# The first gate of a fused transformer kernel: its 16 modulation steps on ScalarE and GpSimd instead of TensorE

## The chip, the cores and the metric

The kernel runs on one core of a Trainium2 chip. The metric is device time in microseconds (us) for one execution of the whole program. The kernel before takes 2242.73 us (median of three runs, 2242.59 to 2245.43).

A core has five engines, each with an instruction queue that is worked off strictly in order: TensorE (PE, matrix products; PEld is its weight load), VectorE (DVE), ScalarE (ACT), GpSimd (POOL) and SyncE (SP, which here only issues DMA transfers). An instruction whose input is not ready holds up everything behind it in its queue.

## The reference, cut to what matters

The program is three transformer layers on 256 tokens of width 2048. Only the first is touched here, and in it only the first gate, `gt1`:

```python
ada = silu(c) @ w_ada + b_ada                 # c: (1, 2048), w_ada: (2048, 6*2048)
sh1, sc1, gt1, sh2, sc2, gt2 = split(ada, 6)
h   = rmsnorm(x, norm1_g) * (1 + sc1) + sh1
proj = h @ w_in                               # 2048 x 3664: q, k, v, index heads, pool
...attention and pooling...
x   = x + gt1 * (mix @ w_out)
h2  = rmsnorm(x, norm2_g) * (1 + sc2) + sh2
x   = x + gt2 * mixture_of_experts(h2)
```

So `gt1` is a row of 2048 numbers: a vector of 2048 times a 2048 x 2048 matrix (16 MB of float32), plus a bias. It is needed on all 128 partitions, since it multiplies the rows of the tokens.

## The kernel before, in words

**Steps.** The first layer is a list of steps (`Dense` objects) that `run_steps` (line 81) goes through. A step has a `first` part (issue the DMA of its weights, and for a projection cast them to a rounded half on ACT), an `end` part (the remainder on DVE) and a `step` part (the products on PE). `first` and `end` are done two steps ahead of `step`. After each step `bg.tick()` emits one piece of each kind of background work: the indexer, the choice of the 64 best keys (`choose`), normed and rotated q and k (`qk_ready`), pooling, attention, and at the end whatever was handed to `bg.later`, one piece of it at every tick.

**Projections.** A projection step (`dense_tok`, lines 489 on; its products are recorded on line 578, its cast on 526, its remainder on 167 like every `tensor_tensor`) takes two blocks of 128 input rows by 512 columns. Each operand is split in a rounded half `h` and a remainder `l`, and three products are made for each of two token halves, 12 in all. Two steps share one load of 1 MB. There are three buffers for the halves (`hp`, line 289), so a cast waits until PE is done with the step three back.

**Modulation steps.** An `ada_step(q, k)` loads one slab, 128 partitions by 2048 columns (1 MB, line 314), and adds `silu(c)` times the slab to a PSUM bank with four matmuls (line 321), side by side on four column groups of 32. A group is 16 steps; `q` is 2 for `gt1`, 3 and 4 for the second shift and scale, 5 for `gt2`. After the sixteenth step of `gt1`, `row` adds the bias and `spread` (line 398) puts the row on all partitions with four matmuls, when the attention phase starts.

**Order.** `merge` lays the modulation steps between projection steps: first `rows[3]` and `rows[4]` (the last two input blocks of the first five column chunks), then `wide` (24 steps for columns 1024 to 1535 and 2640 to 3663), then the 32 steps of `out_steps`, which multiply with `w_out` and need `gt1`.

**Buffers.** All these loads, projection or modulation, take their place from one ring, `raw()` (lines 262 on). In the middle of this phase it has six places of 1 MB: three buffers `w`, the two halves of the tile `X`, and `wx`. From the first step of the last eight of `wide` on it has four, `w, w, w, wx` (line 968), because `X` is about to be loaded again with the tokens; when `attention()` is called, at the end of `wide`, it gets six again with the halves of `big`. SP issues the loads in order: a load waits until its place is free, and all loads behind it wait too.

## Time and profile before

| | |
|---|---|
| median of three runs | 2242.73 us |
| profiled execution: its own time | 2241.87 us |
| its span (first to last instruction) | 2240.1 us |
| PE busy over the span | 1902.8 us (85%) |
| DVE, ACT, POOL busy | 989.3, 629.7, 73.4 us |
| moved by DMA | 694.94 MB |

The page of the profile cuts the span in 40 slices of 56 us. The steps of `gt1` lie in slices 3 to 5 (155 to 232 us) in the kernel before. Slices 11 to 24 are the experts of the first layer, and there the DMA runs at a constant 421 GB/s; from slice 25 on the second and third layers run, which the change doesn't touch. A row of a timeline gives start, duration, engine, source line, operation, the tile written and the tiles read, shape and count, and in brackets how long the engine had sat idle before and what it waited for.

### The profile page before, as it was taken

To read this page: it belongs to the slowest core of one execution; us is meant where nothing else is said; L and a number is where in the kernel's file an instruction comes from. 1 tells how busy PE (TensorE), PEld (TensorE's weight loads), DVE (VectorE), ACT (ScalarE), POOL (GpSimd) and SP (SyncE) were. 2 spreads that over 40 slices of the span, in tenths; PEclk is the share of its full clock that TensorE was granted. 3 is DMA by queue.
4 is the path that set the end of the run, shared out by engine and by line. 5 is a ranking of instruction groups with operands and counts; after the bars stand their busy time and mean duration, and the time that the engine had idled before them with its cause. 6 is when DMAs were issued, how large, how long until landed. Compare 5 with 4: busy or idle time off the path is not lost.

```text
span 2240.1 us, 35046 instructions
## 1 busy us (share of the span) xinstructions
PE 1902.8 (85%) x14718; PEld 1371.0 (61%) x14718; DVE 989.3 (44%) x1866; ACT 629.7 (28%) x1072; POOL 73.4 (3%) x90
## 2 busy tenths in 40 slices
PE   5999999986678676766767685999999999999998
PEld 3666656752234142423233242799989999989986
DVE  2456736531112121121212121667886657556864
ACT  2333324320000000000000010365574444435543
POOL 2000100000000000000000000000000011200000
PEclk9999999998799788898878788999999999999999
DMA  9999898899899999999999999855535556444554
GB/s 334 382 361 339 314 393 295 331 378 416 351 421 421 420 421 421 421 421 421 420 421 418 421 415 421 309 170 175 184 128 177 181 168 182 148 151 151 170 189 149
DMA packets 198065, 694.94 MB, mean 310 GB/s; under 512 B 20454, under 2 KB 44552, under 8 KB 140432
## 3 DMA queue, kind: packets, MB, share of 16 engines
q1 hardware_dynamic: 194608, 682.03, 80.0%
q0 software_dynamic: 2000, 6.89, 1.0%
q10 hardware_dynamic: 1296, 3.74, 0.5%
q8 instruction: 117, 1.92, 0.3%
q14 instruction: 44, 0.36, 0.0%
HBM read 690.49 MB, written 2.11 MB: 309 GB/s over the span
## 4 chain that ended last, share of the span: by engine, by line
PE 41%; DMA 28%; DVE 2%; ACT 1%; issue 1%; SPq 0%; ACTq 0%; POOLq 0%; POOL 0%; DVEq 0%
PE acc L578 29%; DMA w<-in_w_dram 12%; DMA a<-in_w_dram 9%; PE acc L1151 4%; PE acc L1186 3%; DMA wx<-in_w_dram 3%; DMA h<-in_w_dram 2%; PE acc L1216 1%; DVE Og L167 1%; DMA w<-in_l_w_uq_dram 1%; PE acc L1378 1%; PE tps L818 1%; PE tps L781 1%; DMA w<-in_l_w_in_dram 0%; PE tps L1712 0%
## 5 line engine op out<-in xcount | busy, mean ns | idle before, releaser
L578 PE MATMUL acc<-h,h 128*128 128x512 f32 (+1 forms) x1152 | 274.7, 388 | 11.5 <-ACT h L526 4.2
L1186 PE MATMUL acc<-w,Xg 128*32 128x256 f32 x2048 | 213.2, 462 | 66.3 <-DMA w<-in_w_dram 64.7
L578 PEld LDWEIGHTS acc<-h,h 128*128 128x128 f32 x1152 | 203.1, 190 | 87.5 <-issue 21.5
L167 DVE TENSOR_TENSOR s<-s,acc 64x256 f32<-64x256 f32 (+1 forms) x34 | 14.9, 439 | 414.1 <-ACT s L1193 409.7
L1186 PEld LDWEIGHTS acc<-w,Xg 128*32 128x32 f32 x2048 | 91.1, 128 | 163.9 <-DMA w<-in_w_dram 93.2
L167 DVE TENSOR_TENSOR Og<-acc,gt 32x512 f32<-32x512 f32 x124 | 85.2, 687 | 219.9 <-PE acc L1216 218.3
L1193 ACT ACTIVATE s<-acc 64x256 f32<-64x256 f32 x32 | 12.1, 377 | 599.5 <-PE acc L1186 599.5
L1186 PE MATMUL acc<-a,Xg 128*32 128x256 f32 x1408 | 136.1, 452 | 46.2 <-DMA a<-in_w_dram 44.0
L167 DVE TENSOR_TENSOR h<-w,h 128x1024 fp32r<-128x1024 f32 (+2 forms) x104 | 121.6, 1173 | 64.1 <-ACT h L526 63.9
L526 ACT CAST h<-w 128x1024 fp32r<-128x1024 f32 (+2 forms) x104 | 103.6, 1002 | 110.9 <-PE acc L578 51.2
L1186 PEld LDWEIGHTS acc<-a,Xg 128*32 128x32 f32 x1408 | 59.0, 126 | 108.9 <-DMA a<-in_w_dram 60.4
L578 PE MATMUL acc<-a,w 128*128 128x256 f32 x948 | 122.1, 285 | 0.1
L578 PE MATMUL acc<-a,wx 128*128 128x256 f32 x948 | 121.8, 284 | 0.2 <-DVE wx L167 0.2
L1151 PE MATMUL acc<-Ps,x 128*128 128x128 f32 x448 | 100.3, 396 | 25.0 <-DVE Ps L1139 21.8
L578 PE MATMUL acc<-a,h 128*128 128x256 f32 (+1 forms) x924 | 118.8, 284 | 0.4 <-DVE h L167 0.4
L1216 PE MATMUL acc<-w,aT 128*32 128x512 f32 x600 | 83.0, 650 | 42.1 <-DMA w<-in_w_dram 26.0
L1151 PEld LDWEIGHTS acc<-Ps,x 128*128 128x128 f32 x448 | 98.5, 310 | 33.1 <-issue 33.1
L578 PEld LDWEIGHTS acc<-a,wx 128*128 128x128 f32 x948 | 116.4, 191 | 2.5 <-issue 2.0
L578 PEld LDWEIGHTS acc<-a,w 128*128 128x128 f32 x948 | 116.6, 191 | 1.8 <-issue 0.7
L578 PEld LDWEIGHTS acc<-a,h 128*128 128x128 f32 (+1 forms) x924 | 113.5, 191 | 2.1 <-issue 1.3
L578 PE MATMUL acc<-a,gt 128*128 128x256 f32 (+1 forms) x876 | 112.3, 284 | 0.0
L578 PEld LDWEIGHTS acc<-a,gt 128*128 128x128 f32 (+1 forms) x876 | 107.6, 191 | 1.8 <-issue 1.7
(496 smaller groups left out, 2819.6 us busy)
## 6 DMA issues: line engine op xcount, KB each, us to landing
w<-in_w_dram SPq DMA_DIRECT2D x206, 1024.0 KB, 19.8
a<-in_w_dram SPq DMA_DIRECT2D x116, 1024.0 KB, 19.8
w<-in_l_w_in_dram SPq DMA_DIRECT2D x160, 512.0 KB, 4.6
w<-in_w_ada_dram SPq DMA_DIRECT2D x44, 1024.0 KB, 7.6
w<-in_l_w_out_dram SPq DMA_DIRECT2D x64, 512.0 KB, 4.7
h<-in_w_dram SPq DMA_DIRECT2D x29, 1024.0 KB, 19.8
wx<-in_w_dram SPq DMA_DIRECT2D x29, 1024.0 KB, 19.8
w<-in_w_ada_dram SPq DMA_DIRECT2D x30, 512.0 KB, 9.8
```

The lines of the kernel that those rows point to most:

```text
L167: (e or DVE).tensor_tensor(out=o, in0=x, in1=y, op=op)
L526: ACT.copy(h, t)
L578: PE.matmul(out_of(r), lt, rt, start=first and i == 0 and o == 0, stop=last and i == 2, skip_group_check=True)
L781: PE.transpose(p[:, b * 128:(b + 1) * 128], P[h][:, b * 128:(b + 1) * 128], ident)
L818: PE.matmul(p[:, r], q[:, t * 128:(t + 1) * 128], k[:, 0:128 * (t + 1)], start=True, stop=True)
L1151: PE.matmul(b[:, (k - k0) * 128:(k - k0 + 1) * 128], x1[:, t, k:D:16], flat(Ps)[:, t], start=t == 0, stop=t == 1)
L1186: PE.matmul(p1[32 * j:32 * j + 32, 0:256], Xg[:, k, 32 * el:32 * el + 32], w[:, k % 4, (j % 2) * 256:(j % 2) * 256 + 256], start=k == 0, s ...
L1193: ACT.activation(s[0:64], p1[0:64, 0:256], AF.Silu)
L1216: PE.matmul(p2[32 * j:32 * j + 32, :], aT[:, kk % 2, (kk // 2) * 32:(kk // 2) * 32 + 32], down[kk][:, j * 512:(j + 1) * 512], start=kk == ...
L1378: PE.matmul(p, PWT[:, t * 128:(t + 1) * 128], Og[:, n:n + 512], start=True, stop=True)
```

## The change

The 16 steps of `gt1` no longer use PE. Such a step, `gate_step(k)`, loads the same slab of 1 MB through the same ring. Then ACT makes copies of it in eight pieces of 256 columns, each scaled by `silu(c)` of its partition, into two small buffers that are used in turn (`some`; it goes by the name `sel`), and POOL adds each piece to a tile `gt1` of 128 x 2048. The first two pieces come with the step, two more with every tick: so four in the step's own turn, two in the next, two in the one after. At the end the 128 partitions of `gt1` are summed, and the sum put on all of them, by one product with ones (`spread_sum`, four matmuls as before).

The order changes with it: the steps of the other groups (`ada`) are laid at half the rate, and the 16 new steps, `g1`, between: 2 with `rows[3]`, 3 with `rows[4]`, 11 in `wide`. Before the end of `wide` there were 32 modulation steps on PE and are now 17; in the first half of `out_steps` 18 and now 16, in the second 3 and now 4. The selector `sel` is made where `gt2` is spread, not at the start. All loads are still made, each once.

```diff
-        sel = pp.tile([128, 4, 128], F32, name="sel")
         DVE.memset(kc["ones"], 1.0)
-        DVE.memset(sel, 0.0)
-        for j in range(4):
-            DVE.memset(sel[32 * j:32 * j + 1, j], 1.0)
...
+        some = pp.tile([128, 2, 256], F32, name="sel")
+
+        def gate_step(k):
+
+
+            cell = {}
+
+            def prep():
+                cell["w"] = w = raw().rearrange("p k n -> p (k n)")
+                SP.dma_start(w, wada[:, k, 2 * D:3 * D])
+
+            def pieces_of(g, w):
+                for i in range(8):
+                    x, n = some[:, i % 2], slice(256 * i, 256 * i + 256)
+                    ACT.activation(x, w[:, n], AF.Copy, scale=cs[:, k:k + 1])
+                    tt(g[:, n], g[:, n], x, OP.add, POOL)
+                    if i % 2:
+                        yield
+
+            def step():
+                if k == 0:
+                    gate["gt1"] = g = pe.tile([128, D], F32, name="gt1")
+                    POOL.memset(g, 0.0)
+                    POOL.dma_start(g[0:1, :], a["b_ada"][0:1, 2 * D:3 * D])
+                bg.later(pieces_of(gate["gt1"], cell["w"]))
+            return Dense(prep, step)
+
+        def spread_sum(name):
+
+            g = gate[name]
+            for j in range(4):
+                t = tps()
+                PE.matmul(t, kc["ones"], g[:, j * 512:(j + 1) * 512], start=True, stop=True)
+                evac(g[:, j * 512:(j + 1) * 512], t)
+                yield
+
...
-        ada = [ada_step(2, k, row("gt1", lambda: pe.tile([128, 512], F32, name="grow"))) for k in range(16)]
-        ada += [ada_step(3, k, columns(2, lambda: ())) for k in range(16)]
+        g1 = [gate_step(k) for k in range(16)]
+        ada = [ada_step(3, k, columns(2, lambda: ())) for k in range(16)]
...
-        bias_row(2, pe.tile([128, 512], F32, name="brow"))
...
-        order += merge(rows[2], lead[3][3:] + lead[4][:3]) + merge(rows[3], lead[4][3:]) + ada[:2]
+        order += merge(rows[2], lead[3][3:] + lead[4][:3]) + merge(rows[3], lead[4][3:] + g1[:2]) + ada[:2]
         del ada[:2]
-        order += merge(rows[4], ada, 6)
+        order += merge(merge(rows[4], ada, 3), g1[2:5])
...
-        order += merge(wide, ada, 24)
+        order += merge(merge(wide, ada, 12), g1[5:])
...
-            for g in (pool_means(4), pool_mix(), spread("gt1", lambda: gt1_at().rearrange("p t c -> p (t c)")),
+            for g in (pool_means(4), pool_mix(), spread_sum("gt1"),
...
-        order += merge(out_steps[:16], ada, 18) + merge(out_steps[16:], ada, len(ada) - TAIL)
+        order += merge(out_steps[:16], ada, 16) + merge(out_steps[16:], ada, len(ada) - TAIL)
...
+                        next(turn_gate)
                         weights()
```

Three places show how the queues change. Each row is a source line, an operation with the tile written and the tiles read, and the queues that it waits for; a number behind a tile tells one use of a buffer from the next, `in_w_ada_dram` is a modulation load, `in_w_in_dram` a load of `wide`, and `in_w_out_dram` the first load of `out_steps`.

SP, before, from the second-last load of `wide` to the first load of `out_steps`:

```order
L517 DMA w_2226<-in_w_in_dram 128x4x512 [waits DMAHW3_49,PE_49]
L314 DMA w_2243<-in_w_ada_dram 128x2048 [waits DMAHW4_49,DVE_49]
L314 DMA w_2264<-in_w_ada_dram 128x2048 [waits DMAHW5_49,DMAHW1_49,PE_49]
L517 DMA wx<-in_w_in_dram 128x4x512 [waits DMAHW6_49,PE_49]
L314 DMA w_2287<-in_w_ada_dram 128x2048 [waits DMAHW7_49,DVE_49]
L314 DMA w_2308<-in_w_ada_dram 128x2048 [waits DMAHW0_49,PE_49]
L314 DMA w_2314<-in_w_ada_dram 128x2048 [waits DMAHW1_49,PE_49]
L314 DMA wx<-in_w_ada_dram 128x2048 [waits DMAHW2_49,DVE_49]
L989 DMA X<-in_x_dram 128x2x2048
L314 DMA w_2347<-in_w_ada_dram 128x2048 [waits DMAHW3_49,PE_49]
L517 DMA big<-in_w_out_dram 128x4x512
```

SP, after, the same stretch (line 392 is a load of the new `gate_step`, line 310 of another modulation step, 554 a projection):

```order
L554 DMA w_2388<-in_w_in_dram 128x4x512 [waits DMAHW4_49,Activation_49]
L310 DMA w_2408<-in_w_ada_dram 128x2048 [waits DMAHW5_49,DMAHW1_49,DVE_49]
L392 DMA w_2426<-in_w_ada_dram 128x2048 [waits DMAHW6_49,PE_49]
L554 DMA wx<-in_w_in_dram 128x4x512 [waits DMAHW7_49,Activation_49]
L310 DMA w_2472<-in_w_ada_dram 128x2048 [waits DMAHW0_49,DVE_49]
L392 DMA w_2497<-in_w_ada_dram 128x2048 [waits DMAHW1_49,PE_49]
L310 DMA w_2517<-in_w_ada_dram 128x2048 [waits DMAHW2_49,Activation_49]
L310 DMA wx<-in_w_ada_dram 128x2048 [waits DMAHW3_49,DVE_49]
L1025 DMA X<-in_x_dram 128x2x2048
L310 DMA w_2543<-in_w_ada_dram 128x2048 [waits DMAHW4_49,PE_49]
L554 DMA big<-in_w_out_dram 128x4x512
```

The last two loads of `wide`, and the load `w_2517` that stands ahead of the tokens and of `w_out`, waited for PE and now wait for ACT (Activation): their places were those of new steps.

ACT, before, the casts of the last three loads of `wide` (two casts each) and of the first of `out_steps`:

```order
L526 CAST h<-w_2176 128x1024 [waits DVE_49]
L526 CAST h<-w_2226 128x1024 [waits DMAHW7_49,DVE_49]
L526 CAST h<-w_2226 128x1024 [waits DVE_49,PE_49]
L526 CAST h<-wx 128x1024 [waits DMAHW2_49,DVE_49,PE_49]
L526 CAST h<-wx 128x1024 [waits DVE_49,PE_49]
L153 COPY PP<-acc 128x512 [waits PE_49]
L153 COPY qiT<-tps 128x512 [waits PE_49]
L526 CAST h<-big 128x1024 [waits DMAHW1_49,DVE_49]
```

ACT, after, the same stretch (line 397 is a scaled piece):

```order
L563 CAST h<-w_2326 128x1024 [waits DVE_49]
L397 ACTIVATE sel<-w_2306,cs 128x256 [waits DMAHW4_49,Pool_49]
L397 ACTIVATE sel<-w_2306,cs 128x256 [waits Pool_49] x7
L563 CAST h<-w_2388 128x1024 [waits DMAHW0_49,DVE_49]
L563 CAST h<-w_2388 128x1024 [waits DVE_49,PE_49]
L397 ACTIVATE sel<-wx,cs 128x256 [waits DMAHW7_49,Pool_49]
L397 ACTIVATE sel<-wx,cs 128x256 [waits Pool_49] x7
L563 CAST h<-wx 128x1024 [waits DMAHW3_49,DVE_49,PE_49]
L563 CAST h<-wx 128x1024 [waits DVE_49,PE_49]
L397 ACTIVATE sel<-w_2426,cs 128x256 [waits DMAHW2_49,Pool_49]
L397 ACTIVATE sel<-w_2426,cs 128x256 [waits Pool_49] x5
L153 COPY PP<-acc 128x512 [waits PE_49]
```

Between the casts of two loads stand eight pieces, and each of these waits for POOL.

ACT, before, where `rows[4]` begins: the last modulated block of tokens (`h_6` and `h_7`) and the casts of the first two steps of `rows[4]` (`w_1269`):

```order
L153 COPY arow<-ada 128x256
L526 CAST h<-w_1269 128x1024
L157 ACTIVATE rl<-h_6_244,shsck,gsc 128x256
L424 CAST h_6_1288<-rl 128x512
L526 CAST h<-w_1269 128x1024
L157 ACTIVATE rl<-h_7_251,shsck,gsc 128x256
L424 CAST h_7_1302<-rl 128x512
```

ACT, after, the same place; the first cast of `rows[4]` is the last row, and the slabs of the first two new steps are `w_1217` and `X`:

```order
L153 COPY arow<-ada 128x256
L563 CAST h<-wx 128x1024
L157 ACTIVATE rl<-h_6_236,shsck,gsc 128x256
L461 CAST h_6_1255<-rl 128x512
L397 ACTIVATE sel<-w_1217,cs 128x256 x4
L157 ACTIVATE rl<-h_7_243,shsck,gsc 128x256
L461 CAST h_7_1274<-rl 128x512
L397 ACTIVATE sel<-w_1217,cs 128x256 x2
L397 ACTIVATE sel<-X,cs 128x256 x2
L397 ACTIVATE sel<-w_1217,cs 128x256 x2
L397 ACTIVATE sel<-X,cs 128x256 x2
L563 CAST h<-X 128x1024
```

Twelve pieces now stand between the modulated block `h_6` and the first cast of `rows[4]`, which stood ahead of it.

## Rows read from the trace of the kernel before

**Rows 1.** Windows: PE, PEld, DVE, ACT, POOL busy (instructions); granted clock, DMA share, GB/s.

```profile
157.90:191.00 33.10, 31.30 (x179) 22.16 (x176) 20.53 (x40) 12.05 (x16) 0.00 (x0) 1.00 0.95 353
191.00:262.00 71.00, 70.43 (x392) 41.98 (x391) 57.37 (x142) 25.76 (x33) 7.93 (x6) 1.00 0.92 341
262.00:300.00 38.00, 37.56 (x199) 23.52 (x201) 11.53 (x12) 9.62 (x12) 0.00 (x0) 1.00 0.83 304
300.00:336.00 36.00, 32.61 (x164) 20.07 (x157) 12.87 (x20) 11.67 (x18) 1.14 (x2) 1.00 1.02 401
```

**Rows 2.** The page: GB/s of each of the 40 slices.

```profile
GB/s 334 382 361 339 314 393 295 331 378 416 351 421 421 420 421 421 421 421 421 420 421 418 421 415 421 309 170 175 184 128 177 181 168 182 148 151 151 170 189 149
```

**Rows 3.** Timeline, PE: modulation and projection steps late in `wide`.

```profile
283.07 1.06 PE L321 MATMUL ada<-wx,cs 128*32 128x512 f32 x8
284.07 3.01 PE L578 MATMUL acc<-h,h 128*128 128x512 f32 x12
287.01 1.06 PE L321 MATMUL ada<-w,cs 128*32 128x512 f32 x8
288.01 3.01 PE L578 MATMUL acc<-h,h 128*128 128x512 f32 x12
291.95 0.73 PE L578 MATMUL acc<-h,h 128*128 128x512 f32 x2
```

**Rows 4.** Instructions by form, ACT: copies of 128x256, scaled by partition and plain.

```profile
L1281 ACT ACTIVATE a<-X,V 128x256 fp32r<-128x256 f32 x32 | 14.2, 499 | 9.5 <-DVE X L167 4.9 <-DMA w<-in_l_w_in_dram 4.5
L1489 ACT ACTIVATE y<-y 128x256 f32<-128x256 f32 x28 | 11.5, 411 | 11.4 <-DVE y L167 11.4
```

**Rows 5.** Timeline of the third layer, POOL and DVE: two-input operations of both.

```profile
1904.98 1.61 POOL L167 TENSOR_TENSOR xc<-xc,K 128x256 f32<-128x256 f32 x1
1905.91 1.76 DVE L167 TENSOR_TENSOR h<-w,h 128x1024 fp32r<-128x1024 f32 x1
1912.41 3.99 POOL L167 TENSOR_TENSOR y<-xc,K 32x256 f32<-32x256 f32 x4
1916.47 0.81 POOL L167 TENSOR_TENSOR xc<-xc,K 128x256 f32<-128x256 f32 x1
1916.60 1.77 DVE L167 TENSOR_TENSOR wx<-w,wx 128x1024 fp32r<-128x1024 f32 x1
1918.63 1.21 DVE L167 TENSOR_TENSOR h<-w,h 128x1024 fp32r<-128x1024 f32 x1
```

**Rows 6.** Timeline, start of `rows[4]`: transposes of the modulation, `h_6`, first product.

```profile
156.58 0.44 PE L353 MATMUL tps<-K,arow 128*128 128x128 f32 x2
156.94 1.06 PE L321 MATMUL ada<-X,cs 128*32 128x512 f32 x8
158.74 0.62 ACT L424 CAST h<-rl 128x512 fp32r<-128x512 f32 x1
160.13 1.21 PE L578 MATMUL acc<-h,h 128*128 128x512 f32 x4 [0.22 <-DVE h L167]
```

**Rows 7.** Timeline, SP, ACT: the last loads of `wide`, and their casts.

```profile
276.32 0.38 SPq L517 DMA_DIRECT2D w<-in_w_in_dram  x1
281.32 2.00 ACT L526 CAST h<-w 128x1024 fp32r<-128x1024 f32 x2 [4.49 <-DMA w<-in_w_in_dram]
284.20 0.38 SPq L517 DMA_DIRECT2D wx<-in_w_in_dram  x1
290.76 2.00 ACT L526 CAST h<-wx 128x1024 fp32r<-128x1024 f32 x2 [7.44 <-DMA wx<-in_w_in_dram]
```

**Rows 8.** Timeline, from the end of `wide` to the first step of `out_steps`.

```profile
294.60 0.43 SPq L989 DMA_DIRECT2D X<-in_x_dram  x1
296.61 3.01 PE L578 MATMUL acc<-h,h 128*128 128x512 f32 x12
297.12 0.73 SPq L517 DMA_DIRECT2D big<-in_w_out_dram  x1
312.22 1.04 ACT L526 CAST h<-big 128x1024 fp32r<-128x1024 f32 x1 [9.47 <-DMA big<-in_w_out_dram]
```

More of the change, by code (lines that the diff above doesn't have):

```diff
@@ L398, in spread @@
         def spread(name, place):
+            sel = pp.tile([128, 4, 128], F32, name="sel")
+            DVE.memset(sel, 0.0)
+            for j in range(4):
+                DVE.memset(sel[32 * j:32 * j + 1, j], 1.0)
+            yield
             r, g = gate[name], place()
```

## The prediction, on record before the result

> **What bounds the kernel now.** I read the windows first. From 158 to 262 us PE has next to no idle time (70.43 us busy of 71.00 from 191 to 262), at a granted clock of 1.00, while the DMA share is 0.92 to 0.95; DVE is at 57.37 of 71.00, the next to bind [rows 1]. So this stretch is bound by PE, and DMA has some room. From 300 to 336 us DMA is at 1.02 of its share and PE has gaps [rows 1]. The page's line of rates shows what follows: the experts run at a flat 421 GB/s from slice 11 on [rows 2], so their end is fixed by when their loads start, and a shift before them should pass through to the end at full size. I take that as given; if the experts absorbed part of it, every number below would shrink.
>
> The timeline of PE late in `wide` then gives the price of what is removed: a modulation step starts at 283.07, the projection behind it at 284.07; the next pair at 287.01 and 288.01 [rows 3]. A modulation step holds PE for 1.00 us (its 1.06 overlaps the next), a projection step for 2.94 to 3.0.
>
> **What it removes.** 16 steps x 1.00 us = 16.0 us of PE. The four matmuls that spread the row stay, with ones for the selector. Gone too are one DVE addition, a fill and a small DMA on POOL; the selector's five fills move to the experts' start. These I count as nothing, with the experts' loads, which bind there [rows 2], as cover; without it they are some 1 us, two of the copies of rows 4.
>
> **What it adds.** 16 x 8 = 128 pieces, each an ACT copy and a POOL addition of 128x256. The trace has the same copy, scaled by partition: 0.50 us, and a plain one at 0.41 [rows 4]. For POOL's two-input operation of this shape the nearest rows are 0.81 us with little in its way, 1.61 us where a DVE operation was running, and four of 32x256 in 3.99 us, 1.00 each [rows 5]. I take 0.81, the row of this shape with least in its way, and keep 0.41 (POOL never late, ACT's plain copy the limit) and 1.61 as ends. With two small buffers the third piece must wait for the first addition, so a run of 8 pieces holds ACT for 0.50 + 6 x 0.81 + 0.50 = 5.9 us (3.3 to 10.7), a run of 12 for 9.1 us (4.9 to 17.1).
>
> The Trainium skill (GPSIMD Engine Reference, Performance versus the Vector engine) gives 4497 ns for such an addition of 2048 columns; in proportion that is an estimate of 0.56 us for 256, below every row here. By it the two runs would be 4.4 and 6.6 us, and the sum below +9 instead of +14.8.
>
> Neither engine is short of time in total: ACT was busy 25.76 of 71.00 us [rows 1]. What matters is that ACT works in order and that its pieces free the buffers. Four places follow.
>
> *1. Start of `rows[4]`.* Twelve pieces now stand ahead of the cast that the first product needs. Before, the transposes of the last modulation were at 156.58, `h_6` was cast by 159.36 (2.8 later), PE was through with its modulation step at 158.00 and in full swing again at 160.13: a gap of 2.1 us [rows 6]. After, the cast ends 2.8 + 9.1 + 1.0 = 12.9 us behind the transposes (the two operations on `h_7`, 1.2 us, fall into waits for POOL), while PE has 0.4 + 3.0 + 2 x 1.0 = 5.5 us to do. The gap is 7.4: a loss of 5.3 us (2.3 to 13).
>
> *2. 191 to 262 us.* Half of some 15 modulation steps leave, so PE needs about 63 us. About 57 additions come. A DVE remainder of 1.21 us took 1.76 and 1.77 where a POOL operation of this shape ran beside it [rows 5], so a meeting costs DVE 0.55 us. If 23 of 57 meet one (DVE is busy four fifths of the time, but a good part is `choose`, which reads one tensor), DVE needs 57.4 + 12.7 = 70 us. That is the old 71, so 7 of the 8 us are not had: a loss of 7 (0 if none meet; 26 if all 57 do, 57.4 + 31.4 = 89). The queue of POOL counts here too: the choice of keys and the two norms of q and k wait for POOL operations that now stand behind additions, and DVE waits for them with the remainders queued behind; I put that into the upper half of this range.
>
> *3. The ring of four.* The last loads of `wide` before took the places of modulation steps that PE freed: issued at 276.32 and 284.20, their casts began at 281.32 and 290.76, 5.0 and 6.6 us later, both waiting for nothing but the load [rows 7]; and PE reached the second at 291.95 and stopped 0.44 us for its remainder, so there was no slack left even then [rows 3]. Now the load waits until ACT is through with 8 pieces that stand behind the two casts of the load before. From cast to cast: 2.0 for two casts [rows 7] + 5.9 + 5.8 for the load = 13.7 us, where PE has 2 x 3.0 + 1.0 = 7.0 us of work. That loses 6.7 us twice. The load before them, held back in SP's order behind a new step's load, loses about 1; the lead of the casts at the change of ring gives about 1.5 back. Loss: 13 us (5 with 3.3 and a load of 5.0; 26 with 10.7 and 6.6).
>
> *4. End of `wide`.* Before, the tokens were asked for at 294.60 and the first of `w_out` at 297.12, 2.5 us ahead of the end of the last projection (299.62); its cast could begin at 312.22, 12.6 behind that end [rows 8]. After, a modulation load ahead of them in SP's order waits for pieces of which the last two stand behind a copy of the last projection's result: about 0.7 + 1.3 = 2.0 us behind its end. Then six loads of 1 MB (the tokens count two) must pass: 15 us at 421 GB/s [rows 2], 16 at 401 [rows 1], and 1 to 2 for the last to land. That is 18 behind the end instead of 12.6: a loss of 5.5 (3 to 9).
>
> **Sum.** -16.0 + 5.3 + 7 + 13 + 5.5 = +14.8 us, on the profiled execution's 2241.87: 2256.7. The median of the runs lies 0.9 above that execution; with it, 2257.
>
> **The rivals.**
>
> *PE bound and all else hidden (faster).* Place: the ring of four. If ACT ran far enough ahead of PE, the pieces would be over before their buffers are wanted, and the 16.0 us would stand: 2227. For it: PE has no idle time from 191 to 262, and ACT and POOL are mostly idle [rows 1]. Against it: two casts and a load alone are 7.0 us, as long as PE's work on a pair, so the runs of eight pieces would have to cost nothing. It decides where a run takes under about 2 us. Chance 0.13.
>
> *The stalls just eat the gain (no change).* All four places near their lower ends, 2.3 + 3 + 7 + 4 = 16: 2243. For it: the order of magnitude is the same, and a stall at one place gives the loads time to catch up for the next. Against it: places 3 and 4 follow one another through the same queue. Chance 0.14.
>
> *GpSimd is the bound (much slower).* 128 additions at 1.3 us, between the two rows, make 166 us; the stretch from 157 to 300 is 143. That is +23, with place 4 behind it +29: 2271; at 1.61 each it would be 206 us and 2311. For it: 1.61 where DVE works on two tensors beside it [rows 5], and DVE does that in every remainder. Against it: from 262 to 300 DVE is busy only 11.53 of 38 us [rows 1]. Chance 0.16.
>
> The Trainium skill (SBUF — State Buffer, Who interferes with whom) says that a DVE instruction with two SBUF inputs and a GpSimd instruction that reads SBUF exclude each other for the whole instruction. The trace agrees so far: both were longer where they met, 1.76 against 1.21 us and 1.61 against 0.81 us. Taken to its end, this is the rival just priced.
>
> **How the numbers follow.** My forecast has 0.57, the rivals 0.13, 0.14 and 0.16. A measurement of this kernel tells about 0.2%, 4.5 us, from no change. Faster: 0.13; within: 0.14; slower: 0.57 + 0.16 = 0.73. All four lower ends together would give -5.7, all four upper ends +58, neither likely; the range goes from 2236, which takes in most of the case without change and leaves out the fast one, to 2284, inside the third rival. The forecast's own range is 2246 to 2270.
>
> **What would show it.** Right: gaps of PE of some 5 to 7 us before each of the last two loads of `wide`, with ACT's casts waiting for `in_w_in_dram` and SP's load waiting for ACT; a gap of some 7 us where `rows[4]` begins; the first cast of `w_out` about 18 us behind the last projection of `wide`; DVE remainders above 1.21 us where POOL adds; runs of eight pieces of about 6 us on ACT. Wrong: PE as full as before up to the end of `wide`, with the end of `wide` 15 us earlier; or additions near 1.6 us with ACT waiting for POOL from the first step on; or a shift before the experts that is gone at their end.

## The result, and the profile after

| | before | after |
|---|---|---|
| median (range), 4 runs each | 2244.02 us (2242.59 to 2245.43) | 2305.51 us (2301.27 to 2306.11) |
| span of the profiled execution | 2240.1 us | 2303.4 us |
| PE, DVE, ACT, POOL busy | 1902.8, 989.3, 629.7, 73.4 us | 1917.9, 1004.0, 686.7, 187.4 us |

The change is slower by a ratio of 1.0270 (1.0258 to 1.0282): 61 us, where 14.8 were forecast. The windows of the kernel after (columns as in [rows 1]) show where:

```profile
191.00:262.00 71.00, 63.25 (x320) 41.09 (x318) 53.11 (x106) 44.96 (x81) 48.85 (x55) 0.99 0.83 310
262.00:300.00 38.00, 25.70 (x104) 17.60 (x104) 20.93 (x42) 16.68 (x30) 24.26 (x22) 0.82 0.33 117
300.00:336.00 36.00, 22.50 (x85) 14.61 (x84) 7.98 (x8) 15.30 (x26) 13.73 (x18) 0.77 0.72 281
```

No engine is full, and from 262 to 300 us DMA has fallen from 304 GB/s [rows 1] to 117: everybody waits for somebody. Where PE waits, its granted clock is 0.82 and 0.77 instead of 1.00. The page's line of rates shows the dip in slices 4 and 5. The dip in slice 11 (363 GB/s) is not new: the kernel before has it in slice 10 (351) [rows 2], and it comes some 60 us later here.

```profile
GB/s 336 381 319 315 262 183 363 305 229 411 421 363 421 420 421 420 421 421 421 420 421 420 421 416 421 385 185 182 165 146 158 185 177 163 166 146 162 169 183 146
```

Following the same instruction through both timelines splits the 63.3 us of span:

| PE's instruction | before | after | later by |
|---|---|---|---|
| first product of `rows[4]` | 160.13 | 164.57 | 4.4 |
| first transposes of the roped queries | 257.89 | 275.36 | 17.5 |
| end of `wide` | 299.62 | 343.74 | 44.1 |
| first product of `out_steps` | 313.69 | 365.45 | 51.8 |
| spread of the second gate, in the experts | 486.74 | 540.94 | 54.2 |
| end of the span | 2240.1 | 2303.4 | 63.3 |

*Start of `rows[4]`*, timeline of ACT and PE (start, us, instruction, and what ended the idle time before it), the places of [rows 6]. Pieces follow each other at 0.69 us, 0.51 of their own and 0.18 of waiting for GpSimd, and the cast stands behind them:

```profile
161.71 0.51 ACT L397 ACTIVATE sel<-w,cs 128x256 f32<-128x256 f32 x1 [0.17 <-POOL gt L167]
163.49 1.03 ACT L563 CAST h<-X 128x1024 fp32r<-128x1024 f32 x1
164.57 11.38 PE L615 MATMUL acc<-h,h 128*128 128x512 f32 x48 [6.09 <-ACT h L563]
```

*The additions*, all 128 by tile (min/median/max in ns), and who waited for them (us, times):

```profile
L167 POOL TENSOR_TENSOR gt<-gt,sel x128: 711/740/5867, 155.1 to 366.0; 128x256 f32<-128x256 f32 x128
who waited for it (us, times):
  ACT sel L397: 43.6, 67
```

*The rope* (the rotation of queries and keys by their position, on VectorE). The longest addition, timeline of POOL, DVE, ACT and PE:

```profile
266.23 5.33 DVE L164 SCALAR_TENSOR_TENSOR big<-big,r,gq 128x128 f32<-128x128 f32 x20
268.38 5.87 POOL L167 TENSOR_TENSOR gt<-gt,sel 128x256 f32<-128x256 f32 x1
271.49 1.21 DVE L167 TENSOR_TENSOR h<-wx,h 128x1024 fp32r<-128x1024 f32 x1
272.62 1.02 DVE L167 TENSOR_TENSOR rt<-big,K 128x160 f32<-128x160 f32 x4
274.28 0.51 ACT L397 ACTIVATE sel<-w,cs 128x256 f32<-128x256 f32 x1 [6.80 <-POOL gt L167]
276.93 1.03 ACT L563 CAST h<-wx 128x1024 fp32r<-128x1024 f32 x1
278.00 1.23 DVE L167 TENSOR_TENSOR h<-wx,h 128x1024 fp32r<-128x1024 f32 x1 [2.78 <-ACT h L563]
282.93 0.90 PE L774 MATMUL tps<-K,big 128*128 128x128 f32 x3 [7.27 <-DVE big L167]
283.48 5.39 PE L615 MATMUL acc<-h,h 128*128 128x512 f32 x12
```

One addition lasts from 268.38 to 274.25, through VectorE's run of two-input operations. ACT's next piece waits 6.80 us for it, the cast at 276.93 stands behind the piece, VectorE's remainder at 278.00 waits for the cast, the rope's sums stand behind the remainder, and PE waits 7.27 us for these. Its next twelve matmuls, at 283.48, take 5.39 us where twelve take 3.01 in [rows 3]. Four in-order queues hand one delay on.

*The ring of four*, timeline of SP, ACT and PE, the places of [rows 7] and [rows 3]:

```profile
305.67 1.04 ACT L563 CAST h<-w 128x1024 fp32r<-128x1024 f32 x1 [7.16 <-DMA w<-in_w_in_dram]
306.77 8.68 PE L615 MATMUL acc<-h,h 128*128 128x512 f32 x24 [4.15 <-ACT h L563]
313.51 0.51 ACT L397 ACTIVATE sel<-w,cs 128x256 f32<-128x256 f32 x1 [0.19 <-POOL gt L167]
314.05 0.38 SPq L554 DMA_DIRECT2D w<-in_w_in_dram  x1
319.21 1.99 ACT L563 CAST h<-w 128x1024 fp32r<-128x1024 f32 x2 [5.19 <-DMA w<-in_w_in_dram]
332.45 1.99 ACT L563 CAST h<-wx 128x1024 fp32r<-128x1024 f32 x2 [5.21 <-DMA wx<-in_w_in_dram]
```

The load of 314.05 leaves when the eighth piece (313.51 + 0.51) gives its place back, and lands 5.2 us later. Cast to cast takes 13.54 and 13.24 us. PE, after waits of 4 us, takes 8.68 us for 24 matmuls that take 2 x 3.01 in [rows 3]: there the granted clock was 1.00, in these 8.68 us it is 0.67, a mean of stretches at the chip's two levels of 1.2 and 2.4 GHz. The slow clock does not lengthen the turns themselves, since PE waits again behind it, 3.87 us for the next cast.

*End of `wide`*, the places of [rows 8]. The first cast of `out_steps` starts 19.45 us behind the last projection:

```profile
340.75 2.99 PE L615 MATMUL acc<-h,h 128*128 128x512 f32 x12
346.73 0.44 SPq L554 DMA_DIRECT2D big<-in_w_out_dram  x1
363.19 1.04 ACT L563 CAST h<-big 128x1024 fp32r<-128x1024 f32 x1 [14.33 <-DMA big<-in_w_out_dram]
```

*End of `out_steps`*, a place that the prediction did not speak of: PE's first and last product of the router, and SP's last modulation load with the first load of the experts behind it. After, then before:

```profile
473.76 1.87 PE L954 MATMUL tps<-wr,h 128*128 128x36 f32 x16
514.18 1.92 PE L954 MATMUL tps<-wr,h 128*128 128x36 f32 x16
513.82 0.33 SPq L310 DMA_DIRECT2D w<-in_w_ada_dram  x1
514.18 2.38 SPq L1062 DMA_DIRECT2D a<-in_w_dram  x4
```

```profile
424.59 1.87 PE L917 MATMUL tps<-wr,h 128*128 128x36 f32 x16
460.03 1.97 PE L917 MATMUL tps<-wr,h 128*128 128x36 f32 x16 [0.35 <-DVE h L155]
450.59 0.33 SPq L314 DMA_DIRECT2D w<-in_w_ada_dram  x1
451.31 5.96 SPq L1026 DMA_DIRECT2D a<-in_w_dram  x4
```

The router's products span 40.4 us instead of 35.4, and the experts' first load goes out 26.8 us ahead of the second gate's spread instead of 35.4. The experts run at the rate of their loads [rows 2], so what was not loaded by then comes off their end: 9.1 us more. They are lost before the dip in the rates, since the load that ends it is already 63.0 us later (before, then after):

```profile
588.44 1.29 SPq L1026 DMA_DIRECT2D w<-in_w_dram  x3
651.43 1.29 SPq L1062 DMA_DIRECT2D w<-in_w_dram  x3
```

### The profile page after: what moved, and what is told of

Read it like the earlier page. It is cut to its first block, busy times and chain, and to the rows that moved or that the text cites. A ratio compares the mean times of both kernels' runs of the same rounds, so it can differ in the third digit from the quotient of the medians.

```text
span 2303.4 us, 35055 instructions
## 1 busy us (share of the span) xinstructions
PE 1917.9 (83%) x14590; PEld 1379.7 (60%) x14590; DVE 1004.0 (44%) x1865; ACT 686.7 (30%) x1200; POOL 187.4 (8%) x218
## 4 chain that ended last, share of the span: by engine, by line
PE 42%; DMA 25%; DVE 2%; ACT 1%; issue 1%; SPq 0%; POOLq 0%; POOL 0%; ACTq 0%; DVEq 0%
PE acc L615 30%; DMA w<-in_w_dram 13%; DMA a<-in_w_dram 8%; PE acc L1187 4%; DMA wx<-in_w_dram 3%; PE acc L1223 2%; DMA h<-in_w_dram 2%; PE acc L1253 1%; DVE Og L167 1%; PE acc L1415 1%; PE tps L855 1%; PE tps L818 1%; PE tps L1749 0%; PE ada L847 0%; PE tps L1598 0%
## 5 line engine op out<-in xcount | busy, mean ns | idle before, releaser
L615 PE MATMUL acc<-h,h 128*128 128x512 f32 (+1 forms) x1152 | 292.8, 404 | 36.0 <-ACT h L563 22.6
L615 PEld LDWEIGHTS acc<-h,h 128*128 128x128 f32 x1152 | 211.9, 199 | 118.4 <-ACT h L563 31.6
L167 POOL TENSOR_TENSOR gt<-gt,sel 128x256 f32<-128x256 f32 x128 | 114.6, 925 | 215.4 <-ACT sel L397 215.1
L1253 PE MATMUL acc<-w,aT 128*32 128x512 f32 x600 | 94.4, 728 | 43.3 <-DMA w<-in_w_dram 28.2
```

The source lines that it names most:

```text
L167: (e or DVE).tensor_tensor(out=o, in0=x, in1=y, op=op)
L615: PE.matmul(out_of(r), lt, rt, start=first and i == 0 and o == 0, stop=last and i == 2, skip_group_check=True)
L1253: PE.matmul(p2[32 * j:32 * j + 32, :], aT[:, kk % 2, (kk // 2) * 32:(kk // 2) * 32 + 32], down[kk][:, j * 512:(j + 1) * 512], start=kk == ...
```

## The experiments

The theories: **A**, pieces that wait for GpSimd stand in ScalarE's queue ahead of the casts; **B**, a slab holds its place until its eighth piece; **C**, the casts' lead is shorter; **D**, the loads after the reload of X stand in another order. Times are medians; a ratio is to the kernel before, run on the same chip, with its 95% interval (the chips differ by up to 0.1%, so kernels of different chips are compared by ratio).

**no_sums, one_piece, dve_sums, not_in_ring.**

```diff
 no_sums:     -  tt(g[:, n], g[:, n], x, OP.add, POOL)
 one_piece:   -  for i in range(8):        +  for i in range(1):
 dve_sums:    -  ... OP.add, POOL)         +  ... OP.add)
 not_in_ring: -  merge(merge(wide, ada, 12), g1[5:])
              +  merge(merge(wide[:-8], ada, 8), g1[5:]) + merge(wide[-8:], ada, 4)
```

> Leaves out the 128 additions on GpSimd; the scaled copies on ScalarE, the slabs and the order stay (so the gate itself is not summed). Theory A (ScalarE's queue: a piece that waits for its tile to be given back by GpSimd holds the casts of the weights behind it): pieces run back to back at 0.45 us, the stretch from 164 us to the first transpose of the query part gets about 20 us shorter, the 6 to 7 us waits of PE near 276 us go, and the time falls from 2305 to 2255 to 2275 us. Theory B (the slab's place in the ring of weight tiles is held until its last piece, and the pieces are spread over several steps): place times hardly change, the ring of four still takes over 12 us a load, and the time stays at 2290 us or more.

Measured 2270.89 us, 1.0126 (1.0109 to 1.0143): in the range of A. The transposes of the roped queries start at 257.62, 17.7 us earlier, and the first product of `out_steps` at 328.87, 36.6 earlier. Half of the gain lies behind the rope: 13 us up to the cast that is at 305.67 in the change and at 275.02 here, 6 in the two turns of the ring (10.82 and 10.19 us). B's expectation that place times hardly change was wrong too, since pieces also give a place back later when they wait.

> Only the first of the eight pieces of each slab is copied and added; all slabs are still loaded, in the same order, and each place is free again after 0.5 us (so seven eighths of the gate are left out). A and B both: nearly all of the loss goes and the 16 us of the removed PE steps show: 2228 to 2240 us. Theory C (the steps without PE work use up the two steps by which casts run ahead, and shorten the lead of the casts): a part of the loss stays, 2250 us or more, with PE waiting for casts although ScalarE is idle before them.

Measured 2254.73 us, 1.0055 (1.0039 to 1.0072): slower than before though nearly nothing of the gate's work is left. C's number, but not its mechanism: `out_steps` starts at 312.96 us, 0.7 earlier than before, and the second gate's spread at 490.96, 4.2 later. The loss lies behind the place that C speaks of, which led to D.

> The 128 additions go to VectorE in place of GpSimd (about 0.35 us each, 45 us in all, behind what is queued there). Theory A in the form that GpSimd is held up by VectorE's operations with two tiles as inputs: ScalarE's waits for a sum shrink below 20 us of 43.6 and the time falls to 2275 to 2290 us. Theory B: within 8 us of 2305. Rival: VectorE, 77 per cent busy between 157 and 262 us, becomes the queue that all wait in, and the time is 2310 us or more.

Measured 2297.28 us, 1.0242 (1.0225 to 1.0259): within B's 8 us, at their edge, so neither A nor the rival. VectorE, with additions of 0.42 us, is now waited for in GpSimd's stead: ScalarE waited 41.5 us for the sums, and the roped queries start at 278.18. Which of the two adds hardly matters.

> All eleven remaining steps of the first gate are placed ahead of the ring of four places; the last eight projection steps have only steps of the third modulation part between them, as before the change. Theory B: the last loads of the projection follow one another at 7 to 8 us in place of 13.4, worth 18 to 25 us, with a few us given back by the denser first part: 2280 to 2292 us. Theory A: the pieces are as long and wait as long where they are now, beside a fuller VectorE: 2298 to 2315 us.

Measured 2282.38 us, 1.0185 (1.0167 to 1.0203): B. The last eight projection steps are through quickly, but the part ahead is later (roped queries 282.84).

**tail_as_before, at_once, dve_alone, dve_early_tail.** The first makes the loads from the reload of X on the same, place by place, as before the change.

```diff
 tail_as_before: -  merge(merge(wide, ada, 12), g1[5:])   +  merge(merge(wide, ada, 11), g1[5:])
                 -  merge(out_steps[:16], ada, 16)        +  merge(out_steps[:16], ada, 18)
 at_once:        -  if i % 2: yield    +  yield once, after the eighth piece
 dve_alone:      -  ACT.activation(...); tt(...)
                 +  stt(g[:, n], w[:, n], cs[:, k:k + 1], g[:, n], OP.mult, OP.add)
 dve_early_tail: dve_alone, + merge(merge(wide[:-8], ada, 7), g1[5:]) + merge(wide[-8:], ada, 4)
                 + merge(out_steps[:16], ada, 18)
```

> One step of the third modulation part moves from the end of the wide projection into the output projection, so that from the reload of X on every load goes to the same place in the same order as before the change; the first gate is computed as in the change. Theory D (with one step fewer in the output projection the turn of the places has shifted, the last modulation load waits 11 us for its place at the end of the output projection, and the loads of the experts, queued behind it on SyncE, start late): the router's first to last product takes 35.4 us again in place of 40.4, the experts get 7 to 8 us back, and the time falls from 2305 to 2291 to 2296 us. Rival: the expert loads start late only because all of the stage is late; then the time stays within 4 us of 2305, or falls by the 1 us of the moved step.

Measured 2279.83 us, 1.0159 (1.0140 to 1.0179): D, and twice as much as it expected. The router takes 35.45 us again (-5), the experts' part of the gain is 9.7; but 14.0 came by the start of `out_steps` (351.45). With one modulation step less in `wide` the loads fall on other places of the ring. The two turns take as long as in the change (13.43 and 13.10 us); what is gained lies ahead of them. The load before them goes out at 287.25 instead of 298.49, and PE waits 0.41 us at the rope instead of 7.27, as no addition takes more than 2.29 us here. How much each of the two gives is not shown.

```profile
277.76 0.55 PE L774 MATMUL tps<-K,big 128*128 128x128 f32 x3 [0.41 <-DVE big L167]
292.63 1.99 ACT L563 CAST h<-w 128x1024 fp32r<-128x1024 f32 x2 [4.62 <-DMA w<-in_w_in_dram]
```

> All eight pieces of a slab are issued in its own step, in place of two in the step and two with each of the next three. Theory B (what hurts is that a slab's place is held over several steps): loads are issued earlier, and the time falls to 2285 to 2300 us. Theory A (what hurts is what stands in ScalarE's queue ahead of the next cast, and it is the same 5.5 us of pieces, now in one block): the time is 2303 to 2330 us.

Measured 2315.97 us, 1.0324 (1.0307 to 1.0341): A. Giving the place back sooner does not pay for eight pieces in one block ahead of the casts: the roped queries start at 292.07.

> Each piece is one operation on VectorE (slab times the column, plus the sum), so that ScalarE and GpSimd have no part in it and the tile between them is gone; 128 operations of about 0.35 us, 45 us, as many as the additions on VectorE took. Theory A (the price is paid in ScalarE's queue, where pieces stand ahead of the casts): against 2297 us with the additions on VectorE it falls to 2265 to 2282 us. Theory B (the price is the place held until the eighth piece): 2290 to 2300 us, as the pieces still come two in a step.

Measured 2296.43 us, 1.0232 (1.0215 to 1.0249): B's number, for another reason. VectorE is full, 91.53 of 102 us, as the rival of dve_sums had it; an operation took 0.478 us, not 0.35:

```profile
160.00:262.00 102.00, 86.02 (x425) 59.52 (x426) 91.53 (x213) 33.69 (x43) 4.47 (x5) 0.92 0.76 288
```

> One operation on VectorE for each piece, no step of the first gate in the ring of four places, and the loads after the reload of X as before the change. If A, B and D each take their own part, the losses go with their causes and a part of the 16 us of the removed steps shows: 2230 to 2250 us. If VectorE, which has 77 per cent of 157 to 262 us already, cannot take 45 us more there, 2255 us or more.

Measured 2265.11 us, 1.0092 (1.0075 to 1.0109): the second case, VectorE cannot take it. It is the best of the kernels that compute the whole gate away from PE, and slower than before.

**one_piece_tail, half_sums, not_in_ring_tail, other_source.** One_piece_tail and not_in_ring_tail add the order of tail_as_before to their namesakes (with 7 and 4 steps in place of 8 and 4 in the second).

```diff
 half_sums:    +  h = slice(256 * i, 256 * i + 128)
               +  tt(g[:, h], g[:, h], x[:, 0:128], OP.add, POOL)
 other_source: -  ACT.activation(x, w[:, n], ...)
               +  ACT.activation(x, w[:, n] if i == 0 else K[:, 0:256], ...)
```

> One piece of each slab, as in one_piece (2254.7 us), and the loads after the reload of X as before the change, as in tail_as_before. Theory D: the 11 to 13 us between one_piece and the kernel before are the order of those loads, so 2238 to 2245 us: no faster than before, though 16 us of work left PE and next to nothing took its place, because the start of the output projection (312.96 us in one_piece, 313.69 before) waits for its loads. Rival: once the order is right the 16 us show, 2225 to 2232 us.

Measured 2239.30 us, 0.9977 (0.9967 to 0.9986). D: some 17 us of one_piece's time, by ratio, were the order of loads. And removing the 16 PE steps gives 5 us (3 to 7) in this order of steps, not 16, even with seven eighths of their substitute left out. Its windows, PE's waits from 191 to 262 us (in total, times, longest) and its casts show why:

```profile
191.00:262.00 71.00, 66.15 (x347) 44.34 (x346) 61.79 (x142) 31.07 (x44) 15.49 (x14) 1.00 0.86 330
220.00:256.50 36.50, 32.44 (x150) 21.61 (x149) 35.58 (x100) 13.38 (x17) 10.94 (x9) 1.00 1.02 407
262.00:300.00 38.00, 34.03 (x171) 23.64 (x169) 10.19 (x11) 9.86 (x14) 4.55 (x4) 0.96 0.84 322
PE acc L615 <- DVE h L167: 4.5, 7, 1.2
278.63 1.99 ACT L563 CAST h<-w 128x1024 fp32r<-128x1024 f32 x2 [8.17 <-DMA w<-in_w_in_dram]
286.30 2.00 ACT L563 CAST h<-wx 128x1024 fp32r<-128x1024 f32 x2 [5.26 <-DMA wx<-in_w_in_dram]
310.41 1.04 ACT L563 CAST h<-big 128x1024 fp32r<-128x1024 f32 x1 [12.74 <-DMA big<-in_w_out_dram]
```

PE now idles 5 and 4 us where it was full [rows 1]. From 191 to 262 us it waits seven times for a remainder from VectorE, which is itself full: 35.58 of 36.50 us from 220 on. So the transposes of the roped queries start only 2.2 us earlier than before (255.70), with eleven modulation products fewer ahead of them. From 262 on the last casts still wait for their loads: the second begins 4.5 us earlier than in [rows 7], the first cast of `out_steps` 1.8 earlier than in [rows 8]. PE, VectorE up to the rope and the turning of the places behind it were bounds of nearly the same height.

> Each addition on GpSimd takes 128 of its piece's 256 columns (so half of the gate is not summed); the copies and their number stay. Pace theory (GpSimd's 0.74 us an addition against 0.45 us a copy makes ScalarE wait): an addition takes about 0.4 us, the waits go, and the time comes near that without sums (2271 us): 2268 to 2280 us. Lock theory (GpSimd loses its time where VectorE reads two tiles, by the meeting and not by the column): 2288 to 2302 us.

Measured 2288.75 us, 1.0197 (1.0180 to 1.0214): the lock theory's range, at its edge. An addition is down to 0.462 us and the waits to 25.8, yet only half of the gain of no_sums is there. So the pace is not all.

> The change with no first-gate step in the ring of four places and with the loads after the reload of X as before. If the two losses are apart (23 us and 25 us): 2255 to 2263 us. If both are paid in the same stretch, the one between the rope and the first weights of the output projection, they overlap: 2264 to 2276 us.

Measured 2270.42 us, 1.0124 (1.0104 to 1.0145): the two losses overlap.

> Pieces two to eight of each slab copy a resident tile of constants in place of the slab, so that the work of ScalarE and GpSimd and its order are those of the change, but the slab's place is free after its first piece (the gate is not the reference's). Theory B (places held): the ring of four goes back to about 8 us a load and the time falls to 2272 to 2290 us. Theory A (only the queue of ScalarE and the sums matter): 2298 to 2310 us.

Measured 2287.70 us, 1.0191 (1.0174 to 1.0209): B, with the work of ScalarE and GpSimd unchanged. Casts in the ring follow each other at 11.4 and 8.0 us:

```profile
304.27 1.04 ACT L563 CAST h<-w 128x1024 fp32r<-128x1024 f32 x1 [2.81 <-DMA w<-in_w_in_dram]
315.64 1.99 ACT L563 CAST h<-w 128x1024 fp32r<-128x1024 f32 x2 [2.62 <-DMA w<-in_w_in_dram]
323.59 1.99 ACT L563 CAST h<-wx 128x1024 fp32r<-128x1024 f32 x2
```

**before_shifted, no_sums_tail, copies_elsewhere_tail.** The last two are no_sums, and no_sums with other_source, in the order of tail_as_before; the first is the kernel before in the order of the change.

```diff
 before_shifted: -  merge(wide, ada, 24)              +  merge(wide, ada, 25)
                 -  merge(out_steps[:16], ada, 18)    +  merge(out_steps[:16], ada, 16)
```

> The kernel before the change, first gate on PE, with one step of the modulation moved from the output projection into the wide projection, so that all loads after the reload of X stand in the order and at the places that they have after the change. Theory D (the turn of the places at the end of the output projection costs 12 to 15 us whatever computes the gate): 2255 to 2259 us. Rival (the order costs only where ScalarE's pieces have made the stage late): 2242 to 2247 us.

Measured 2258.96 us, 1.0064 (1.0043 to 1.0084), 14 us: D, with the gate on PE. Here too the last modulation load waits for its place until the end of the router, and the experts behind it:

```profile
470.27 0.33 SPq L314 DMA_DIRECT2D w<-in_w_ada_dram  x1
470.64 2.20 SPq L1026 DMA_DIRECT2D a<-in_w_dram  x4
```

> All copies on ScalarE, no additions on GpSimd (so the gate is not summed), and the loads after the reload of X as before the change. It stands between one_piece_tail (2239.3 us) and tail_as_before (2279.8 us): if the additions are the larger part, as no_sums says (35 of 2305 us), 2246 to 2256 us; if copies that hold a place are the larger part, 2258 to 2270 us.

Measured 2250.06 us, 1.0031 (1.0022 to 1.0041): the additions are the larger part.

> As no_sums_tail, but the second to eighth copy of each slab read a resident tile, so that the slab's place is free after its first copy (the gate is not computed). Theory B (held places): what no_sums_tail takes above one_piece_tail goes, 2238 to 2243 us. Theory A (copies stand in ScalarE's queue ahead of casts): it stays, within 3 us of no_sums_tail.

Measured 2242.05 us, 0.9997 (0.9988 to 1.0007): B for the most part; a rest of 4 us (1 to 7) above one_piece_tail fits A.

**one_input, small_sums.** The first takes the second tensor from VectorE's run beside the long addition; the second is half_sums with 32 columns.

```diff
 one_input: -  stt(qk[:, t, h], qk[:, t, h], r10[:, t, h:h + 1], gq[:, h // 8], OP.mult, OP.mult)
            +  DVE.tensor_scalar(out=qk[:, t, h], in0=qk[:, t, h], scalar1=r10[:, t, h:h + 1],
            +                    scalar2=None, op0=OP.mult)
```

> The change, with the twenty operations on VectorE that scale the query and key heads reading one tile in place of two (the norm's weight vector is left out of them). Lock theory: GpSimd's addition of 5.87 us beside this run of 5.33 us goes back below 1.8 us, ScalarE's wait of 6.80 us below 2, and with what stands behind it the time falls by 4 to 9 us: 2296 to 2302 us. Rival (that addition was long for another reason, or PE's wait at the rope is made elsewhere): an addition of over 3 us is still there, or the time stays within 2 us of 2305.

Measured 2301.70 us, 1.0273 (1.0254 to 1.0292). The traces bear out the lock's mechanism: the long addition is gone. Its price is not settled. By ratio nothing is gained, with an uncertainty of 5 us; in the profiled executions the span is 4.7 us shorter (2298.7) and the first product of `out_steps` 4.5 earlier. Six additions beside the run now take 4.15 us, 0.69 each, and the longest is 2.94, beside the remainder and the rope that follow:

```profile
265.42 7.12 DVE L767 TENSOR_SCALAR big<-big,r 128x128 f32<-128x128 f32 x20
267.52 4.15 POOL L167 TENSOR_TENSOR gt<-gt,sel 128x256 f32<-128x256 f32 x6
L167 POOL TENSOR_TENSOR gt<-gt,sel x128: 712/740/2938, 155.5 to 361.3; 128x256 f32<-128x256 f32 x128
360.91 3.47 PE L615 MATMUL acc<-h,h 128*128 128x512 f32 x12
```

But the run takes 7.12 us instead of 5.33, and ScalarE still waits 4.79 and 2.65 us there, where the expectation had waits below 2.

> Each addition on GpSimd takes 32 of its 256 columns. If the cost of the additions goes by the column (128 columns gave back 16.8 of 34.6 us): 2273 to 2278 us. If about half of it comes with the addition itself, as its start, its handshake with ScalarE and its meetings with VectorE: 2283 to 2289 us.

Measured 2281.65 us, 1.0176 (1.0159 to 1.0193), between the two. Of the 0.0144 that no_sums gives, 32 columns give 0.0094; the other third, 11 us, comes with the addition however short it is. Its trace has two waits of ScalarE for a sum above 1.1 us, 7.08 and 3.09, both at the rope:

```profile
L167 POOL TENSOR_TENSOR gt<-gt,sel x128: 242/254/5382, 155.1 to 340.1; 128x32 f32<-128x32 f32 x128
```

**The ladder.** All but the last have the loads from the reload of X on in the order of before, and each adds one thing to the one above; us are differences of ratios times 2244. (The first still has one copy and one addition for each slab; the second has no additions.)

| kernel | ratio | adds | us |
|---|---|---|---|
| one_piece_tail | 0.9977 | 16 PE steps gone, one piece a slab | -5 |
| copies_elsewhere_tail | 0.9997 | copies in ScalarE's queue | +4 |
| no_sums_tail | 1.0031 | places held by the copies | +8 |
| tail_as_before | 1.0159 | additions on GpSimd | +29 |
| the change | 1.0270 | its order of loads | +25 |

Each step has an uncertainty of 3 to 5 us. The order by itself costs 14 (before_shifted), and 14 with no gate step in the ring of four (not_in_ring against not_in_ring_tail). It costs 17 with one piece, 21 with the copies alone and 25 in the change. So the other 11 go with the pieces in the ring; whether by held places or by the addition of 5.87 us, which tail_as_before lacks, stays open.

## Why the prediction was wrong

The direction was right and so was the mechanism at places 1, 3 and 4; the size was not. The steps that failed are the gain of 16.0 us, place 2, the size of place 3, and the order of loads behind place 4, which the sum left out. What places 2 and 3 are said to have measured below is counted against the full 16.0 us, so the 11 us of it that were not had lie largely inside them.

*What it removes: -16.0, measured -5.* The step counted PE's time in full because PE had no idle time [rows 1]. The rows held the objection: VectorE was named as next to bind, the last casts waited for nothing but their loads [rows 7], and PE had no slack against them [rows 3]. Without seven eighths of the pieces PE waits for VectorE up to the rope and for loads behind it (one_piece_tail). Where bounds are of nearly equal height, taking one away gives little.

*Place 1: +5.3, measured +4.4.* Right; pieces came at 0.69 us instead of 0.81.

*Place 2: +7, measured about 23.* This is the step whose mechanism failed, though 23 lies inside its range. From the first product to the roped queries the stretch grew by 13.0 us, with ten modulation products fewer, 1.00 us each. The prediction priced meetings of VectorE and GpSimd on VectorE's own time. They were paid in ScalarE's queue, through waits of 4.99 and 6.80 us around the norms of the queries and keys (the queue that the prediction put into its upper half), and shorter ones at half of the pieces (67 waits in all). At the first of the two, GpSimd still had a norm's operation of 2.90 us ahead of the additions:

```profile
260.18 0.51 ACT L397 ACTIVATE sel<-w,cs 128x256 f32<-128x256 f32 x1 [4.99 <-POOL gt L167]
```

Without the additions the roped queries start at 257.62 (no_sums). GpSimd was no bound: an addition took 0.74 us in the median, and GpSimd was busy 48.85 of 71.00 us. So the third rival had nearly the time of its 1.61 us case (2311) and not the mechanism.

*Place 3: +13, measured about 32.* From the roped queries to the end of `wide` the stretch grew by 26.7 us with five modulation products fewer. The turn itself was predicted well (13.7; 13.54 and 13.24), but the loss was looked for in the two turns, and they hold 6.1 of the 26.7. 18.1 lie ahead of the cast at 305.67, whose counterpart before is

```profile
270.11 1.05 ACT L526 CAST h<-w 128x1024 fp32r<-128x1024 f32 x1 [0.80 <-DMA w<-in_w_in_dram]
```

Some 2 of them are transposes with `band` that stood behind this cast before. Missing in the sum were PE's 7.27 us at the rope, the clock behind that wait (5.39 us for 3.01 of work), and most of the wait for the load ahead of the two turns. It was priced at about 1; its cast waited 7.16 us, because the load left at 298.49, behind a slab's load that an eighth piece had held back until 298.04.

*Place 4: +5.5, measured +6.9.* Right: 19.45 us behind the last projection, predicted 18.

*Behind place 4: taken as a shift at full size, measured +11.5 on top.* One step fewer for `out_steps` was read as a count. It turned the places by one, so that the last modulation load waited and the experts' loads behind it. With the part ahead of `out_steps`, which lies in place 3, the order costs 25 us (tail_as_before), the largest thing that the sum left out.

The GpSimd estimate of the Trainium skill (GPSIMD Engine Reference, Performance versus the Vector engine), 0.56 us by proportion, lay below the 0.74 of the trace. Additions of 32, 128 and 256 columns took 0.254, 0.462 and 0.740 us: 2.17 ns a column and 0.185 us besides, which proportion leaves out. Carried on to 2048 columns that is an estimate of 4.63 us, 3% above the 4497 ns of that section.

What stays open: the 29 us of the additions are by two thirds their length (small_sums against no_sums), and the third that stays fits the two waits at the rope, but one_input, which took the longest meeting away, cannot tell a gain of 4 us from none. No kernel that computes the whole gate away from PE beat the kernel before, and the 5 us of one_piece_tail, with most of the gate left out, leave little room for one in this order of steps.

## What to carry to other kernels

Work that is moved to an idle engine costs what it delays in that engine's queue, and how long it holds its input: here 12 us for the copies alone, against 5 us gained, on an engine that was busy 25.76 of 71.00 us before [rows 1] and 50.70 with the copies (no_sums_tail). Before counting a removed step at full price, look at what the waits next to it end on: a full engine, the next fullest engine and a full ring of buffers can be of nearly one height. When an edit changes how many loads come ahead of a stage, write out which place each later load gets; one step's shift cost 14 us by itself.

## What the hardware showed that was not expected

An addition on GpSimd beside VectorE's two-input operations did not end after one of them. It ran 5.87 us, from 268.38 to 274.25, while VectorE went without a gap from the run of twenty (to 271.56) to a remainder and the rope; with 32 columns, 0.254 us in the median, one still took 5.38. At_once, one_piece and other_source each have an addition of 5.86 or 5.87 us too. Beside twenty one-input operations additions kept 0.69 us. The Trainium skill (SBUF — State Buffer, Who interferes with whom) has the loser wait for the whole instruction; the trace agrees on who blocks whom and shows a wait over many instructions in a row.

PE's clock followed its waits: 1.00 from 262 to 336 us in the kernel before [rows 1], 0.82 and 0.77 in the change, where PE waited 4 to 7 us at a time.
